# A new opening, other places for the modulation rows, and one update for all latents of a block

## The chip, the core and the metric

The kernel runs on one core of one Trainium2 chip. The metric is device time in microseconds (us) of one launch, the median of several executions. Engines are named as in the profile: PE is TensorE's matmul stream and PEld its weight loads, DVE is VectorE, ACT is ScalarE, POOL is GpSimd, and SP is the engine whose queue issues all DMAs of this kernel. L289 is line 289 of the kernel before.

## What is computed

Two layers of a diffusion backbone over 128 context tokens and 512 latent tokens, with a model width of 1024. Cut to what matters here:

```python
def ada_params(cvec, w_ada, b_ada):
    m = jax.nn.silu(cvec) @ w_ada + b_ada
    return jnp.split(m[:, None, :], 6, axis=-1)     # sh1, sc1, g1, sh2, sc2, g2

def modulate(x, g, shift, scale):
    return rms_norm(x, g) * (1 + scale) + shift

for l in range(DEPTH):
    sh1, sc1, g1, sh2, sc2, g2 = ada_params(c, w_ada[l], b_ada[l])
    h = modulate(x, norm_g[l, 0], sh1, sc1)
    y = mixer(h)                  # l = 0: pooling and gated convolution; l = 1: attention
    x = x + g1 * y
    h = modulate(x, norm_g[l, 1], sh2, sc2)
    x = x + g2 * swiglu(h, w_ffn_in[l], w_ffn_out[l])
```

Context tokens take one conditioning vector, latents another, so each modulation parameter has two columns.

## The kernel before, in words

Features lie on the 128 partitions, tokens along the free axis: `x` is 8 blocks (`k`) of 128 features by 640 columns, 128 of context and 512 of latents. Every fp32 product is made of three fp32r products: both operands are split by `pair` (L144, L145) into a high part (a copy on ACT) and a low part (the rest, on DVE), and hi·hi, hi·lo and lo·hi are summed in PSUM.

**Matmuls of a block.** `block_mm` (L283 to L296) makes one block of 128 output features. For each `k` and each of the three products it issues two matmuls with the same weights, one for columns 0 to 320 into one PSUM bank, one for columns 320 to 640 into the next bank. With `ext` (input projections) the second takes two more columns, the shift that goes through the weights with the tokens. Without `ext` it serves the output projections: `po` of layer 0, `wa` and `wb` of layer 1, and `fo` of both FFNs. The last two blocks of the last `fo` have a loop of their own (L1490), with all 384-column matmuls of a block first and then all 256-column ones, over the same `x` layout. The fast products of the FFN input (L632) put 12 matmuls of 320 columns one after the other into one bank.

**PSUM.** Blocks take turns in three PSUM tiles of two banks each, so a block's matmuls wait for what reads the block three turns before.

**Residuals.** When a block is done, `residual` and `update` (L508) add gate times block to `x[:, k]` with three DVE operations: context (128 columns), latents in the first bank (192) and latents in the second bank (320).

**Modulation parameters.** A part (shift, scale, gate; 8 blocks of 128) of layer 0 is made in one of two ways. In the opening, TensorE makes a chunk of 512 parameters from four DMAs of 512 KB of `w_ada` (`ada_pe`, L306: 16 matmuls with 2 columns of weights and 512 moving), ACT copies the result (L324), TensorE turns it (`ada_turn`, L330: 8 matmuls), and DVE adds the bias and makes the scale (L394, L403). All other blocks are rows of the class `AdaDve` (L372): per row one DMA of 512 KB and, on DVE, a multiply-and-sum with SiLU of the conditioning, `silb`. A row is two DVE pieces of 1024 elements in the mixer stage (`junk` in SBUF) and four of 512 in the FFN (`junk` in PSUM). Where rows are run is written by hand: `each` says how many rows go with a block. The first `EARLY` rows run in the opening, `pi` and `po`; 48 run in layer 0's FFN.

**The opening** (L774 to L904) is written by hand, in order, for every engine. Before, it loads the whole scale of layer 0's first norm (chunks 2 and 3), then half the shift (chunk 0); the other half of the shift is the first four rows on DVE. `prep` (L485, L487) makes bufA[k] = x[k] times scale. `first_mm` makes the first three blocks of `pi` as the pieces of `x` come. `nrm.finish` gives `rstd`, in two halves of columns. `scaled_main` (L523) takes a block out of PSUM as `ev`, `first_bias` and `first_turn` (L875, L888) add the shift to the first three blocks. `turn_over` (L815) is filler work on zeros. `ws.load` and `ws.split` load and split projection weights.

**Order.** Outside the opening a planner that knows the dependences orders each engine's work, by program order and readiness; a row is held behind the operation that was traced before it on its engine. `pi` is 16 blocks (3 in the opening, 13 in `project`), four for pooling (`s`, `pl`), twelve for the convolution. `po` is 8 blocks. Then comes the FFN in three groups (8, 8 and 6 hidden blocks, `gi` 0 to 2): input products, then 8 output blocks `fo` with rows beside them.

Of the kernel before, what the change touches and what calls it, by code (L numbers as in the profile page):

```python
# [36 lines left out]
EARLY = 28  # L37
# [23 lines left out]
def hybrid_step(  # L61
# [9 lines left out]
    wada0,  # L71
    wada,
# [209 lines left out]
    def block_mm(ps, w, rhs, kn, ext=False, mcol=0, k0=0, ks=None):  # L282
# [197 lines left out]
    def prep(k, dst, l, n):  # L480
        assert (l, 3 * n + 1, 4 if (l, 3 * n + 1, 4) in known and k < 4 else 8) in known
# [74 lines left out]
    def project(name, rhs, kn, n, done, ext=False, each=None, start=0):  # L556
        for i in range(start, n):
            ps = ps_tile(f"{name}_{i}")
            w = ws.next()
            if each:  # L560
                each(i)
            pipe.step(lambda: block_mm(ps, w, rhs, kn, ext=ext), lambda: done(i, ps))
# [192 lines left out]
    with tc.tile_pool(name="pool1", bufs=1) as p1:  # L755
# [6 lines left out]
        def ada_load(ch):  # L762
            for q in range(4):
                raw = p0.tile([P, 2, 512], F32, tag="araw", bufs=6, name=f"raw_ada{ch}_{q}")
                nc.sync.dma_start(raw, wada0[(ch + 1) // 2 if ch < 3 else 2, q])
                ada_raw.append(raw)
# [4 lines left out]
            [(0, 4, 4)]  # L771
            + [(0, 8 * p, 8) for p in (2, 4, 3)]
# [17 lines left out]
        ada.load()  # L790
        ada.load()
        pwr = p0.tile([P, 512], F32, tag="pwr", name="pwr").rearrange("p (g c) -> p g c", g=4)
        nc.sync.dma_start(pwr, pw)
        ws.load(3)
        zero = p0.tile([P, 512], F32, tag="junk", name="zero")
# [21 lines left out]
        turn_over(6)  # L817
        acc = {ch: ada_acc(ch) for ch in (2, 3)}
        ada_pe(2, acc[2], range(4))
        row = ada_row(2, acc[2])  # L820
        turn_over(3)
        ada_turn(2, row)
        turn_over(14)
        for k in range(4):
            prep(k, bufA, 0, 0)
            if k == 1:
# [4 lines left out]
        first_mm(0, range(4))  # L831
        ada_pe(3, acc[3], range(4))
        row = ada_row(3, acc[3])
        nrm.add_square(V)
        nrm.add_square(V)
        nrm.add_square(V)
        nrm.add_square(V)
        first_mm(1, range(2))
# [52 lines left out]
        first_mm(2, range(5, 6))  # L891
# [3 lines left out]
        first_mm(2, range(6, 8))  # L895
# [147 lines left out]
        for m in range(3):  # L1043
# [9 lines left out]
            each=lambda i: ada.run(1 + (5 <= i < 8)),  # L1053
# [19 lines left out]
        with tc.tile_pool(name="pool4", bufs=1) as p4:  # L1073
            ada.home(p4, p1, 2, ps_small("junk"), silb)
            ada.limit = len(ada.todo)
            ada.load()
            ada.load()
            more = tuple(p4.tile([P, 3 * 4 * HT], F32R, tag=t, name=t) for t in ("x0h", "x0l"))
            ffn(
                0,  # L1080
                bufA,
                bufA,
                each=lambda i, gi, plain=False: ada.run(0 if plain else 1 + (i % 2 if gi == 0 else int(i > 1))),
                fast_each=lambda gi, n, p: ada.run(int(p == 6 and gi > 0)),
                last=last0,
                spare=(tuple(t.rearrange("p a b -> p (a b)") for t in bufB), more),
            )
            assert ada.at == len(ada.todo)
# [4 lines left out]
    with tc.tile_pool(name="pool2", bufs=1) as p2:  # L1093
# [282 lines left out]
        def pieces(name, rhs, kn, todo, cuts, ext, done, share=1, k0=0):  # L1376
# [3 lines left out]
            def piece(i, c):  # L1380
# [5 lines left out]
                block_mm(box["ps"], box["w"], rhs, kn, ext, i % share, k0, range(c * n, c * n + n))  # L1386
# [57 lines left out]
        for m in range(2):  # L1444
            pipe.step(lambda: block_mm(fw[m], wpart[0], bufB, 4, mcol=m, k0=4, ks=range(3)))
        assert not pipe.due
        out_done = updater(1, 16, Norm("b1"), (bufA, 1, 1))
        for m in range(2):
            pipe.step(lambda: block_mm(fw[m], wpart[0], bufB, 4, mcol=m, k0=4, ks=(3,)), lambda: out_done(m, fw[m]))
        for m in range(2, KB):  # L1450
            if not m % 2:
# [3 lines left out]
                lambda: block_mm(ps, wpart[0], bufB, 4, mcol=m % 2, k0=4), lambda: out_done(m, ps)  # L1455
# [58 lines left out]
    gates = AdaDve([(1, 40 + b, 1) for b in range(8)], 76)  # L1514
# [59 lines left out]
_ADA_ORDER = [4, 5, 6, 7]  # L1574
_ADA_ORDER += [8 * p + b for p in (2, 4, 3, 5, 7, 6, 8, 10, 9, 11) for b in range(8)]
# [63 lines left out]
```

## Time and profile before

| | |
|---|---|
| median of 3 runs | 1356.52 us (1354.65 to 1358.49) |
| profiled execution, its own time | 1359.17 us |
| its span, first to last instruction | 1357.0 us |
| granted TensorE clock, mean | 0.993 of full |
| PE, DVE, ACT, POOL busy | 98, 79, 47 and 3% of the span |

Time stamps count from the first instruction. The opening ends at about 57 us, `pi` at 156.6, `po` at 213; layer 0's FFN ends at about 663, attention lies between 720 and 880, layer 1's FFN follows. A row of the timeline is start, duration, engine, line, operation, out<-in, shape and count; square brackets give the idle time of the engine before it and what ended it. Matmul ends are modelled and overlap the next start, so the pace of a stream is read from starts.

### The profile page before, as it was taken

The page shows a single profiled execution, that of the slowest core. Times are in us where ns is not written, and L with a number is a line of the kernel's source. Part 1 is how long each engine was busy: PE and PEld are TensorE (multiplying, and loading weights), DVE is VectorE, ACT ScalarE, POOL GpSimd, SP SyncE. Part 2 cuts the span into 40 slices and gives each one's busy share as a digit, 9 for nine tenths or more (in the row PEclk, how much of TensorE's full clock was granted, in tenths as well). Part 3 has the DMA queues.
Part 4 walks back from the last instruction along what each step waited for, and adds up shares of the span by engine and source line. Part 5 has one row for each costly group of instructions (what it writes and reads, how often), then busy time and mean ns, then how long its engine had stood idle before and what let it go on. Part 6 is the DMA issues. An engine that isn't in the chain of part 4 may idle for free.

```text
span 1357.0 us, 22469 instructions
## 1 busy us (share of the span) xinstructions
PE 1327.6 (98%) x8952; PEld 1295.8 (95%) x8952; DVE 1076.8 (79%) x2095; ACT 638.5 (47%) x1159; POOL 46.3 (3%) x56
## 2 busy tenths in 40 slices
PE   9999999999999999999999999999999999999996
PEld 6899999999999999999998999999999999999995
DVE  4899897978999999999877677599877777446744
ACT  5433245753145521554666675477541355314543
POOL 0000000000000000000012221000000000000001
PEclk9899999999999999999999999999999999999998
DMA  9735422115433454344431110141144122311212
GB/s 366 284 109 190 168 94 94 63 63 171 171 124 111 156 189 151 124 135 161 148 101 48 48 48 32 34 154 47 47 140 164 39 94 70 118 63 63 78 47 78
DMA packets 36808, 155.54 MB, mean 115 GB/s; under 512 B 3936, under 2 KB 11104, under 8 KB 25952
## 3 DMA queue, kind: packets, MB, share of 16 engines
q1 hardware_dynamic: 36704, 154.12, 32.8%
q8 instruction: 70, 1.15, 0.3%
q14 instruction: 34, 0.28, 0.1%
HBM read 148.60 MB, written 2.88 MB: 112 GB/s over the span
## 4 chain that ended last, share of the span: by engine, by line
PE 82%; DVE 11%; ACT 3%; issue 2%; DMA 1%; SPq 0%; POOL 0%; DVEq 0%; ACTq 0%; POOLq 0%
PE fi L632 28%; PE fo L289 19%; PE fi L289 8%; PE pi L289 7%; PE pq L289 5%; PE po L289 4%; DVE junk L372 3%; PE wb L289 2%; PE wa L289 2%; PE o L1355 2%; PE s L1305 2%; DVE wl_fi_p L145 1%; PE t L1338 1%; ACT wh_fi_p L144 1%; DMA x<-xT 1%
## 5 line engine op out<-in xcount | busy, mean ns | idle before, releaser
L144 ACT ACTIVATE wh_fi_p<-raw_fi 128x512 fp32r<-128x512 f32 x252 | 154.5, 626 | 232.0 <-PE fi L632 123.6
L372 DVE CUSTOM_DVE_ANT_0 junk<-rawa,silb 128x512 f32<-128x512 f32 (+1 forms) x280 | 224.1, 800 | 5.9 <-DMA rawa<-wada 1.7
L145 DVE TENSOR_TENSOR wl_fi_p<-raw_fi,wh_fi_p 128x512 fp32r<-128x512 f32 x252 | 171.4, 687 | 65.0 <-ACT wh_fi_p L144 65.0
L144 ACT ACTIVATE wh_fo<-raw_fo 128x1024 fp32r<-128x1024 f32 (+1 forms) x48 | 47.5, 990 | 147.4 <-PE fo L289 122.8
L508 DVE SCALAR_TENSOR_TENSOR x<-fo,mod,x 128x128 f32<-128x128 f32 (+1 forms) x144 | 55.8, 434 | 70.4 <-PE fo L289 67.2
L632 PE MATMUL fi<-bh,wh_fi_p 128*128 128x320 f32 x288 | 88.8, 308 | 1.8 <-DVE x L508 1.8
L632 PE MATMUL fi<-bh,wl_fi_p 128*128 128x320 f32 x288 | 88.9, 309 | 0.0
L632 PE MATMUL fi<-ah,wl_fi_p 128*128 128x320 f32 x288 | 88.7, 308 | 0.0
L632 PE MATMUL fi<-al,wh_fi_p 128*128 128x320 f32 x288 | 88.7, 308 | 0.0
L632 PE MATMUL fi<-ah,wh_fi_p 128*128 128x320 f32 x288 | 88.5, 307 | 0.0
L632 PE MATMUL fi<-bl,wh_fi_p 128*128 128x320 f32 x288 | 88.4, 307 | 0.0
L289 PE MATMUL fo<-al,wh_fo 128*128 128x320 f32 x352 | 80.8, 310 | 0.0
L289 PE MATMUL fo<-ah,wh_fo 128*128 128x320 f32 x352 | 80.6, 310 | 0.1
L289 PE MATMUL fo<-ah,wl_fo 128*128 128x320 f32 x352 | 80.4, 309 | 0.0
L289 PE MATMUL fo<-bh,wh_fo 128*128 128x320 f32 x328 | 75.2, 310 | 0.0
L289 PE MATMUL fo<-bh,wl_fo 128*128 128x320 f32 x328 | 75.0, 310 | 0.0
L289 PE MATMUL fo<-bl,wh_fo 128*128 128x320 f32 x328 | 74.9, 310 | 0.0
L632 PE MATMUL fi<-x0h,wh_fi_p 128*128 128x320 f32 x216 | 68.1, 320 | 1.5 <-ACT fi L644 0.9
L632 PE MATMUL fi<-xh,wh_fi_p 128*128 128x320 f32 x216 | 67.9, 320 | 0.2
L632 PE MATMUL fi<-xh,wl_fi_p 128*128 128x320 f32 x216 | 66.5, 309 | 0.0
L632 PE MATMUL fi<-xl,wh_fi_p 128*128 128x320 f32 x216 | 66.5, 309 | 0.0
L632 PE MATMUL fi<-x0h,wl_fi_p 128*128 128x320 f32 x216 | 66.4, 308 | 0.0
(372 smaller groups left out, 3786.7 us busy)
## 6 DMA issues: line engine op xcount, KB each, us to landing
raw_fi<-wfi SPq DMA_DIRECT2D x44, 1024.0 KB, 4.7
rawa<-wada SPq DMA_DIRECT2D x84, 512.0 KB, 3.4
raw_fo<-wfo SPq DMA_DIRECT2D x16, 1024.0 KB, 4.9
raw_ada<-wada SPq DMA_DIRECT2D x12, 512.0 KB, 7.3
raw_in<-win SPq DMA_DIRECT2D x6, 1024.0 KB, 5.3
raw_fo<-wfo SPq DMA_DIRECT2D x8, 768.0 KB, 4.2
raw_qkv<-wqkv SPq DMA_DIRECT2D x6, 1024.0 KB, 5.4
raw_out<-wout SPq DMA_DIRECT2D x4, 1024.0 KB, 5.2
```

Source lines behind the costliest of these rows:

```text
L144: S.activation(h, src, AF.Copy)
L145: eng.tensor_tensor(out=l, in0=src, in1=h.bitcast(F32), op=ALU.subtract)
L289: PE.matmul(ps[:, h, 0 : hi - lo], w[a][:, k, cols], rhs[b][:, k0 + k, lo:hi], start=k == 0 and a == b, stop=k == kn - 1 and a == 1,)
L372: op = V.tensor_tensor_reduce(out=self.junk, in0=raw[:, cols], in1=self.silb[:, c, cols], scale=1.0, scalar=0.0, op0=ALU.mult, op1=ALU.add ...
L508: V.scalar_tensor_tensor(out=xs, in0=got[:, 0 : b - a], scalar=mod[l][:, gate0 + m, c : c + 1], in1=xs, op0=ALU.mult, op1=ALU.add,)
L632: PE.matmul(out, w[a][:, k, :], ops.get(OPERAND[p], b)[:, k, :], start=fresh and k == 0 and a == b, stop=k == ops.kn - 1 and a == 1, skip_ ...
L1305: PE.matmul(self.ps[:, hf, 0:HT], bufB[a][:, self.h, q0 : q0 + P], kt[b][:, self.kv, hf * HT : hf * HT + HT], start=n == 0, stop=n == 2,)
L1338: PE.transpose(flat(pt)[:, s * P : s * P + P], self.pe[:, s * P : s * P + P], ident)
L1355: PE.matmul(po[:, 0 : 2 * P], vt[a][:, self.kv, s * P : s * P + P], got[b][:, s, :], start=s == 0 and n == 0, stop=s == 4 and n == 2,)
```

## The change

- The scale's first half (blocks 0 to 3) is made in two half chunks of 256 parameters, each from two DMAs (`wadah`, `ada_load_half`, `ada_half`, `ada_half_turn`), so `x` comes in pieces of 2, 2 and 4 blocks; the DMA order is new; win1 is loaded ahead of both shift chunks.
- The whole shift of layer 0's first norm is made on TensorE (chunks 0 and 1). The four rows on DVE are gone; `EARLY` is 24 instead of 28. SiLU of `silb` and the first two rows move to the end of the opening.
- `first_mm(2, ...)` is cut finer and partly moved ahead of the shift chunks.
- Rows with `pi`: 1, 0, 0, 1, 0, 1, 2, 1, 2, 1, 2, 1, 2 instead of 1, with 2 in the sixth to eighth. Rows with layer 0's `fo`: group 0 has 14 instead of 12, group 1 has 12 instead of 14, with 1 and 0 in its last two blocks instead of 2 and 2.
- Without `ext`, `block_mm` cuts at column 384 instead of 320, so each bank holds 256 latents, and `residual` updates all 512 latents with one DVE operation of two runs of 256.

```diff
-EARLY = 28
+EARLY = 24
+PI_ROWS = (1, 0, 0, 1, 0, 1, 2, 1, 2, 1, 2, 1, 2)
...
+    CUT = CTX + LAT // 2
-        span = ((0, 0, HT), (1, HT, TX if ext else T))
+        span = ((0, 0, cut), (1, cut, TX if ext else T))
...
     def residual(ps, m, l, gate0):
-        parts = ((0, 0, CTX, ps[:, 0]), (1, CTX, HT, ps[:, 0, CTX:]), (1, HT, T, ps[:, 1]))
-        update(m, l, gate0, parts)
+        update(m, l, gate0, [(0, 0, CTX, ps[:, 0])])
+        xs = halves(x[:, m, CTX:T])
+        V.scalar_tensor_tensor(
+            out=xs,
+            in0=flat(ps)[:, CTX : CTX + 768].rearrange("p (a b) -> p a b", a=2)[:, :, 0 : LAT // 2],
...
-        ada_load(2)
+        ada_load_half(0)
         nc.sync.dma_start(kc, konst)
-        nc.sync.dma_start(x[:, 0:4, :], xT[:, 0:4, :])
+        nc.sync.dma_start(x[:, 0:2, :], xT[:, 0:2, :])
         ws.load(1, cut=True)
+        ada_load_half(1)
+        nc.sync.dma_start(x[:, 2:4, :], xT[:, 2:4, :])
         ada_load(3)
         nc.sync.dma_start(x[:, 4:8, :], xT[:, 4:8, :])
+        ws.load(2, cut=True)
+        ada_load(0)
+        ada_load(1)
         nc.sync.dma_start(silb, crows[None].broadcast_to((P, 2, D)))
-        ada.load()
-        ada.load()
-        ada_load(0)
-        ws.load(2, cut=True)
-        ada.load()
-        ada.load()
         nc.sync.dma_start(pwr, pw)
         ws.load(3)
+        for _ in range(4):
+            ada.load()
...
-        turn_over(6)
-        acc = {ch: ada_acc(ch) for ch in (2, 3)}
-        ada_pe(2, acc[2], range(4))
-        row = ada_row(2, acc[2])
-        turn_over(3)
-        ada_turn(2, row)
-        turn_over(14)
-        for k in range(4):
+        turn_over(4)
+        row = ada_half(0)
+        turn_over(3)
+        ada_half_turn(0, row)
+        turn_over(10)
+        for k in range(2):
             prep(k, bufA, 0, 0)
...
+        first_mm(0, range(2))
+        row = ada_half(1)
+        first_mm(1, range(1))
+        ada_half_turn(1, row)
+        first_mm(1, range(1, 2))
+        for k in range(2, 4):
+            prep(k, bufA, 0, 0)
...
-        S.activation(silb, silb, AF.Silu)
+        ws.split(2, ahead=False)
...
-        ada.run(1, hold=False)
...
-        ada.run(1, hold=False)
-        ws.split(2, ahead=False)
-        ada.run(2, hold=False)
-        S.preload_act_table_set("natural_log_exp_and_others")
+        first_mm(2, range(0, 2))
         acc = ada_acc(0)
         ada_pe(0, acc, range(4))
         row = ada_row(0, acc)
+        S.preload_act_table_set("natural_log_exp_and_others")
+        first_mm(2, range(2, 3))
+        ada_turn(0, row)
         nrm.finish((0, HT), None)
-        first_mm(2, range(0, 1))
-        ada_turn(0, row)
-        first_mm(2, range(1, 5))
+        first_mm(2, range(3, 4))
+        acc = ada_acc(1)
+        ada_pe(1, acc, range(4))
+        row = ada_row(1, acc)
+        first_mm(2, range(4, 5))
+        ada_turn(1, row)
         prep_shift(bufA, 0, 0)
...
+        S.activation(silb, silb, AF.Silu)
         ws.split(4, ahead=False)
+        ada.run(2, hold=False)
         startup.close()
...
-            each=lambda i: ada.run(1 + (5 <= i < 8)),
+            each=lambda i: ada.run(PI_ROWS[i]),
...
-                each=lambda i, gi, plain=False: ada.run(0 if plain else 1 + (i % 2 if gi == 0 else int(i > 1))),
+                each=lambda i, gi, plain=False: ada.run(0 if plain else (1, 2, 1, 2, 2, 2, 2, 2)[i] if gi == 0 else (1, 2, 2, 2, 2, 2, 1, 0)[i]),
```

## Rows read from the trace of the kernel before

**Rows 1.** The page: busy time of each engine, share of the span, instructions.
```profile
PE 1327.6 (98%) x8952; PEld 1295.8 (95%) x8952; DVE 1076.8 (79%) x2095; ACT 638.5 (47%) x1159; POOL 46.3 (3%) x56
```
**Rows 2.** Waits of PE: who was waited for, us in total, times, longest.
```profile
PE pi L289 <- ACT ev L528: 2.1, 1, 2.1
PE fi L632 <- DVE x L508: 1.8, 1, 1.8
...
PE fi L632 <- ACT fi L644: 0.9, 1, 0.9
```
**Rows 3.** Busy time by stretch: length, each engine, granted clock (PEclk), DMA share, GB/s.
```profile
41.00:47.60 6.60, 6.60 (x27) 6.60 (x28) 6.36 (x14) 1.18 (x3) 0.00 (x0) 0.50 1.02 410
...
81.90:85.30 3.40, 3.40 (x15) 3.40 (x14) 3.40 (x7) 0.00 (x0) 0.00 (x0) 0.51 0.44 159
```
**Rows 4.** Timeline of the opening, PE.
```profile
24.31 0.95 PE L330 MATMUL adat<-kc,row 98*128 98x2 f32 x8
...
34.90 2.27 PE L306 MATMUL adap<-raw_ada,silc 128*2 128x512 f32 x16
...
38.97 0.55 PE L289 MATMUL pi<-ah,wh_in 128*128 128x320 f32 x2 [0.74 <-ACT wh_in L144]
...
40.90 0.90 PE L289 MATMUL pi<-ah,wl_in 128*128 128x320 f32 x2 [1.09 <-DVE wl_in L145]
```
**Rows 5.** Timeline from the opening to the third block of project, DVE and ACT.
```profile
29.34 1.90 ACT L843 ACTIVATE silb<-silb 128x2048 f32<-128x2048 f32 x1
...
38.93 1.28 ACT L856 ACT_TABLE_LOAD   x1
...
55.87 0.68 DVE L145 TENSOR_TENSOR bl<-pwr,bh 128x512 fp32r<-128x512 f32 x1
57.94 1.23 DVE L145 TENSOR_TENSOR wl_in<-raw_in,wh_in 128x1024 fp32r<-128x1024 f32 x1 [1.39 <-ACT wh_in L144]
...
67.80 1.22 DVE L372 CUSTOM_DVE_ANT_0 junk<-rawa,silb 128x1024 f32<-128x1024 f32 x1
...
79.79 0.82 DVE L523 TENSOR_TENSOR ev<-pi,rstd 128x640 f32<-128x640 f32 x1
```
**Rows 6.** Timeline of layer 0's FFN where a group's output ends, PE and DVE.
```profile
363.85 1.14 DVE L508 SCALAR_TENSOR_TENSOR x<-fo,mod,x 128x128 f32<-128x128 f32 x3 [1.32 <-PE fo L289]
...
377.78 0.31 PE L632 MATMUL fi<-bh,wh_fi_p 128*128 128x320 f32 x1
...
379.79 0.55 DVE L508 SCALAR_TENSOR_TENSOR x<-fo,mod,x 128x320 f32<-128x320 f32 x1
...
536.23 0.46 PE L626 MATMUL fi<-bh,onesr 128*128 128x320 f32 x2
...
539.57 0.55 DVE L508 SCALAR_TENSOR_TENSOR x<-fo,mod,x 128x320 f32<-128x320 f32 x1
```
**Rows 7.** The page: two groups, with busy us, mean ns, idle time before them.
```profile
L372 DVE CUSTOM_DVE_ANT_0 junk<-rawa,silb 128x512 f32<-128x512 f32 (+1 forms) x280 | 224.1, 800 | 5.9 <-DMA rawa<-wada 1.7
...
L508 DVE SCALAR_TENSOR_TENSOR x<-fo,mod,x 128x128 f32<-128x128 f32 (+1 forms) x144 | 55.8, 434 | 70.4 <-PE fo L289 67.2
```
**Rows 8.** Timeline of PE: first matmuls of streams of different width.
```profile
156.59 0.46 PE L289 MATMUL po<-bh,wh_out 128*128 128x320 f32 x2
...
213.24 0.46 PE L289 MATMUL fi<-ah,wh_fi 128*128 128x320 f32 x2
...
434.10 0.31 PE L632 MATMUL fi<-bh,wh_fi_p 128*128 128x320 f32 x1
...
437.60 0.36 PE L632 MATMUL fi<-bh,wh_fi_p 128*128 128x320 f32 x1
...
1331.80 0.34 PE L1490 MATMUL fo<-bh,wh_fo 128*128 128x384 f32 x1
...
1338.09 0.28 PE L1490 MATMUL fo<-bh,wh_fo 128*128 128x256 f32 x1
...
1340.10 0.28 PE L1490 MATMUL fo<-bh,wl_fo 128*128 128x256 f32 x1
```

More of the change, by code (lines that the diff above doesn't have):

```diff
@@ L71, in hybrid_step @@
     wada0,
+    wadah,
     wada,
@@ L480, in prep @@
     def prep(k, dst, l, n):
-        assert (l, 3 * n + 1, 4 if (l, 3 * n + 1, 4) in known and k < 4 else 8) in known
+        assert any((l, 3 * n + 1, m) in known for m in range(k + 1, 9))
         h, lo = dst
@@ L556, in project @@
     def project(name, rhs, kn, n, done, ext=False, each=None, start=0):
+        cut = HT if ext else CUT
         for i in range(start, n):
@@ L561, in project @@
                 each(i)
-            pipe.step(lambda: block_mm(ps, w, rhs, kn, ext=ext), lambda: done(i, ps))
+            pipe.step(lambda: block_mm(ps, w, rhs, kn, ext=ext, cut=cut), lambda: done(i, ps))
     def updater(l, gate0, nrm, then):
@@ L764, in ada_load, with ada_load_half @@
                 raw = p0.tile([P, 2, 512], F32, tag="araw", bufs=6, name=f"raw_ada{ch}_{q}")
-                nc.sync.dma_start(raw, wada0[(ch + 1) // 2 if ch < 3 else 2, q])
+                nc.sync.dma_start(raw, wada0[min(ch, 2), q])
+                ada_raw.append(raw)
+        def ada_load_half(half):
+            for q in range(2):
+                raw = p0.tile([P, 4, 256], F32, tag="araw", bufs=6, name=f"raw_adah{half}_{q}")
+                nc.sync.dma_start(raw, wadah[half, q])
                 ada_raw.append(raw)
@@ L815, in turn_over, with ada_half @@
                 PE.matmul(idle, zeror, zeror2, start=True, stop=True)
-        turn_over(6)
-        acc = {ch: ada_acc(ch) for ch in (2, 3)}
-        ada_pe(2, acc[2], range(4))
-        row = ada_row(2, acc[2])
+        half_acc = ada_acc("h")
+        def ada_half(half):
+            out = half_acc[:, 256 * half : 256 * half + 256]
+            for q in range(2):
+                raw = ada_raw.pop(0)
+                for j in range(4):
+                    PE.matmul(
+                        out[32 * j : 32 * j + 2, :],
+                        silc[:, 4 * q + j, :],
+                        raw[:, j, :],
+                        start=False,
+                        stop=q == 1,
+                        tile_position=(0, 32 * j),
+                        skip_group_check=True,
+                    )
+            row = tmp(f"rowh_{half}")[0:98, 0:256]
+            S.activation(row, out[0:98, :], AF.Copy)
+            return row
@@ new lines, in ada_half_turn @@
+        def ada_half_turn(half, row):
+            ps = ps_small(f"adath_{half}")
+            for b in range(2):
+                PE.matmul(
+                    ps[:, 2 * b : 2 * b + 2],
+                    row[:, b * P : b * P + P],
+                    kc[0:98, C_SUM : C_SUM + 2],
+                    start=True,
+                    stop=True,
+                )
+            ada_done(0, 8 + 2 * half, ps[:, 0:4].rearrange("p (b c) -> p b c", c=2))
+        turn_over(4)
+        row = ada_half(0)
@@ L829, in hybrid_step @@
         for k in range(4):
             nrm.square(k)
[L831 to L838, printed above, removed]
+        first_mm(0, range(2, 4))
+        acc = ada_acc(3)
+        ada_pe(3, acc, range(4))
+        row = ada_row(3, acc)
+        for _ in range(4):
+            nrm.add_square(V)
+        first_mm(1, range(2, 4))
@@ L1385, in piece @@
                 n = kn // cuts
-                block_mm(box["ps"], box["w"], rhs, kn, ext, i % share, k0, range(c * n, c * n + n))
+                block_mm(box["ps"], box["w"], rhs, kn, ext, i % share, k0, range(c * n, c * n + n), HT if ext else CUT)
                 if c == cuts - 1:
@@ L1444, in hybrid_step @@
         for m in range(2):
-            pipe.step(lambda: block_mm(fw[m], wpart[0], bufB, 4, mcol=m, k0=4, ks=range(3)))
+            pipe.step(lambda: block_mm(fw[m], wpart[0], bufB, 4, mcol=m, k0=4, ks=range(3), cut=CUT))
         assert not pipe.due
@@ L1448, in hybrid_step @@
         for m in range(2):
-            pipe.step(lambda: block_mm(fw[m], wpart[0], bufB, 4, mcol=m, k0=4, ks=(3,)), lambda: out_done(m, fw[m]))
+            pipe.step(lambda: block_mm(fw[m], wpart[0], bufB, 4, mcol=m, k0=4, ks=(3,), cut=CUT), lambda: out_done(m, fw[m]))
         for m in range(2, KB):
@@ L1454, in hybrid_step @@
             pipe.step(
-                lambda: block_mm(ps, wpart[0], bufB, 4, mcol=m % 2, k0=4), lambda: out_done(m, ps)
+                lambda: block_mm(ps, wpart[0], bufB, 4, mcol=m % 2, k0=4, cut=CUT), lambda: out_done(m, ps)
             )
@@ L1513, in hybrid_step @@
     S.activation(silb, silb, AF.Silu)
-    gates = AdaDve([(1, 40 + b, 1) for b in range(8)], 76)
+    gates = AdaDve([(1, 40 + b, 1) for b in range(8)], 72)
     gates.home(p3, p3, 2, ps_small("junk1"), silb)
@@ L1571 @@
 _FFN_ORDER = [b + j for j in range(FB) for b in (0, FB)]
-_ADA_ORDER = [4, 5, 6, 7]
-_ADA_ORDER += [8 * p + b for p in (2, 4, 3, 5, 7, 6, 8, 10, 9, 11) for b in range(8)]
+_ADA_ORDER = [8 * p + b for p in (2, 4, 3, 5, 7, 6, 8, 10, 9, 11) for b in range(8)]
 _SHAPES = (
```

33 lines of the change are left out of this document (18 added, 15 removed).

## The prediction, made before the change was run

> **What bounds the kernel now.** I read the busy times first: TensorE is busy for 98% of the span [rows 1]. So time is won only where TensorE waits, runs at its lower clock, or issues its stream at another pace; what VectorE (DVE) saves counts only where TensorE waits for it. Next, TensorE's waits by name [rows 2]: 2.1 us in the input projection for ACT's `ev`, 1.8 us in layer 0's FFN for the residual, 0.9 us beside it for ACT's `fi`. Then the stretches, for the granted clock [rows 3]: 0.50, its level of 1.2 GHz, from 41.0 to 47.6 us, and again from 81.9 to 85.3. Before each fall TensorE had waited: twice before the first [rows 4], 2.1 us at the projection's third block before the second. Last, the timelines around these places: a clock fall and a wait belong to the opening, and the two FFN waits stand where one group's output ends.
>
> **The opening, DMA order.** Up to chunk 3 the queue carries the same bytes in both kernels, only in other pieces, so `x[4:8]` comes when it came before. win1 is moved past silb, two rows and chunk 0, about 4.2 MB; at the 410 GB/s of a full queue [rows 3] it lands some 10 us earlier. Behind it, chunks 0 and 1, silb, pwr, win2 and four rows come later. Chunk 1's last two parts need buffers that TensorE frees in chunk 0, and all behind them on SP's queue wait too. I cost that at nothing: win2 is first needed by the second block of `project`, and pwr and the rows after the opening; if that cover goes, TensorE waits for win2 by the delay itself.
>
> **The opening, TensorE.** Gone are the waits for win1's parts, 0.74 + 1.09 = 1.8 us [rows 4], and with them the cause I see for the first clock fall: 6.60 us at half pace [rows 3] cost 3.3 us. The two half chunks stream as many columns as the chunk they replace. New is chunk 1 on TensorE: 2.27 us of matmuls and a turn of 0.95 [rows 4], 3.2 us. That leaves 1.9 us; up to 3.3 if finer pieces of `x` also hide the wait for chunk 3, which no row prices.
>
> **The opening, DVE and ACT.** I doubt that this gain reaches TensorE. The third block of `project` starts only when `ev` of its first convolution block is out of PSUM, and the row of that `ev` starts at 79.79 after DVE has been in arrears since the opening's end [rows 5]. The four shift rows that leave DVE ran before that, where DVE could spare them except beside win1. In their place SiLU of silb moves to the end, ahead of `wh_in` on ACT, with `wl_in` behind it on DVE: 1.90 us, and since ln and exp were loaded in between, a table load of 1.28 [rows 5], 3.2 us. Two rows, four pieces, also stand there, and one row comes with the first block: six pieces ahead of that `ev`, where the timeline has five, so 1.2 us more. Sum on this path: 3.2 + 1.2, less the 1.39 us that DVE idles there anyway [rows 5], less the 1.9 to 3.3 us that it starts earlier: +1.1 to -0.3 us, if the idle is filled. I take 0. Ends: -3.3, if nothing binds behind TensorE, and 3.2 + 1.2 - 1.9 = +2.5, if no idle is filled. The wait of 2.1 us grows to some 4 or 5 us, and I expect the second clock fall to stay.
>
> The Trainium skill (ScalarE: Activation LUTs, What ACT_TABLE_LOAD costs) speaks against this move: it puts a switch of table sets at 2.66 us, the load and a drain of 1.38. By it the opening would end 1.4 us later, and the sum would be -1.7 instead of -3.1; the row has the 1.28 us alone.
>
> **Rows beside `pi`.** 14 instead of 16 there and 2 instead of 4 in the opening. TensorE shows no wait for them in the later blocks, so 0; the cover is the three PSUM tiles. If DVE falls two blocks behind, a wait of up to a row's two pieces, 2.4 us [rows 5], comes back.
>
> **Rows in the FFN.** Group 1 loses two rows near its end, eight pieces of 0.80 [rows 7], 6.4 us of DVE. Its last residual ended at 540.12, 3.9 us after the output's last matmul [rows 6]; now it follows at once, and the waits of 1.8 and 0.9 us go [rows 2]: -2.7. Group 0 gets these two rows. Its last residual ended at 380.34, 2.6 us after the output [rows 6], and TensorE went on then without a wait. How late it gets is bounded twice: 6.4 us less the 1.32 that DVE idles there [rows 6], 5.1; or, by the group that has had 14 rows so far, 3.9 - 2.6 = 1.3. I take the second, the same blocks with the same number of rows, less about half for the shorter residuals: +0.6. Ends 0 and 5.1. Together -2.1.
>
> **One update.** It drops one of three operations whose busy time is 0.39 each (55.8/144) [rows 7], but moves the same elements, so 0 to 0.39 us per block. DVE is ahead of TensorE at these blocks but in the two places above, so 0 elsewhere.
>
> **The cut at 384.** This one touches most of the kernel: `fo`, `po`, `wa`, `wb`, 2808 matmuls, 1404 pairs, counted from the loops. The 384 matmuls of `po` take 213.24 - 156.59 = 56.65 us [rows 8], 147.5 ns each, 295.0 a pair. At L1490, 36 of 384 columns take 6.29 us, 174.7 each; 17 steps of 256 columns take 2.01, 118.2 each [rows 8]: 292.9 a pair, 2.1 ns less, -2.9 us over 1404. But those rows keep to one bank, and `block_mm` changes banks every time. In the fast products, which keep to one bank with 320 columns, 24 take 3.50 us, 145.8 each [rows 8], 291.6 for two: by them the new widths cost 1.3 ns a pair, +1.8 us. L1490 shares widths and layout with the changed blocks, the other stream does not, so I lean to it: -1.0, ends -2.9 and +1.8.
>
> The Trainium skill (TensorE: Matmul & The Clock Gate, Back-to-back issue gap) gives a gap of N/2.4 + 2.5 ns, 271.7 for either pair: by it the cut is worth 0 and the sum is -2.1. The rows are 8% slower than it, so it cannot decide a per cent.
>
> **Sum.** 0 - 2.1 - 1.0 = -3.1 us. The profiled execution took 1359.17 us, 2.17 more than its span; the start and end around the span don't change. 1359.17 - 3.1 = 1356.1. Its own time lies 2.65 above the median of the runs, so I give 1353.4 on the median's scale. 0.3%, about what a measurement of this kernel can tell from no change, is 4.1 us.
>
> **Rivals.**
> *The opening counts in full.* If the planner lays the two early rows behind the pool sums, DVE and ACT don't bind. For it: DVE loses a whole row in each of several blocks after. Against it: `ev` at 79.79. -3.3 - 2.1 - 1.0: 1350.1.
> *The FFN wait only moves.* Group 0's last residual has no slack, and 5.1 us late is a bound, so a wait of 2.7 there would cancel group 1's gain: 1355.5. Against it: group 1's own lateness.
> *Slower: the short half is bound by its weight load.* Each matmul reloads weights, and PEld is 95% busy [rows 1]. Behind a 384-column matmul the 256-column one may not keep 118.2 ns. From 295.0 - 174.7 + 1.5 = 121.8 ns the whole change loses; at 128 it is 9.8 above the row, and the time is 1359.17 - 2.65 - 2.1 + 1404 x 7.7 ns = 1365.2. Against it: L1490's stream keeps 118.2 for a whole block.
> *The clock falls in the new opening.* It feeds TensorE in pieces of two blocks, with waits for DMA between. The rows have a fall after such waits; one more of 6.6 us costs 3.3: 1356.7. The Trainium skill (TensorE: Matmul & The Clock Gate, HAM oscillation) says that idle gaps between bursts put the clock back to its lower level; the trace agrees, with 0.50 after the waits at 39 and 79 us.
>
> **Chances.** Forecast 0.48, opening in full 0.19, moved wait 0.17, short half 0.09, clock 0.07. Faster by over 0.3% means below 1352.4: the full opening and a third of the forecast, 0.36. Slower, above 1360.6: the short half, 0.09. Same: 0.55. The range, 1348.8 to 1358.0, takes in all but the short half and the far ends of the bounds: the low end is the full opening with part of the cut's -2.9, the high end the forecast with the opening at +2.5 and the cut at +1.1.
>
> **What would show it.** PE's waits: no L508 or `fi` wait near 536, one of under 1 us near 380, the one for `ev` L528 grown to 4 or 5 us. Clock: no fall near 41, one near 82. Pace: pairs of 384 and 256 at 294 ns. Wrong would be: `ev`'s wait no longer than 2.1 us, pairs under 292.9 or over 296.3, or a wait over 2 us after group 0.

## The result, and the profile after

The changed kernel takes 1361.17 us (median of 9 runs, 1359.86 to 1362.41), the kernel before 1358.07 beside it (9 runs, 1354.65 to 1359.38): ratio 1.0025, 95% interval 1.0016 to 1.0034. The forecast was 1353.4 us in a range of 1348.8 to 1358.0. So the change costs 3.4 us where 3.1 were to be won. (The forecast stood on a median of 1356.52 us from 3 runs; 1.6 us of its distance to the result lie in that base.) The profiled execution spans 1359.1 us, against 1357.0 before.

First the page, busy time by engine; then PE's waits (who was waited for, us in total, times, longest).

```profile
PE 1330.0 (98%) x8987; PEld 1298.0 (96%) x8987; DVE 1060.2 (78%) x2011; ACT 640.3 (47%) x1162; POOL 46.4 (3%) x56
```
```profile
PE py L1020 <- ACT ev L544: 2.8, 2, 2.6
...
PE pi L295 <- ACT ah L491: 2.0, 2, 1.5
PE pi L295 <- DVE bl L1029: 1.8, 1, 1.8
PE pi L295 <- DVE al L493: 0.5, 2, 0.2
...
PE fi L643 <- DVE x L528: 0.4, 1, 0.4
PE fi L649 <- ACT fi L661: 0.4, 1, 0.4
```

The FFN's waits of 1.8 and 0.9 us behind group 1 [rows 2] are gone; the 0.4 for `x` is new and stands behind group 0, the 0.4 for `fi` is new too, in layer 1's FFN at 965.81 us. In the projection one wait of 2.1 became two, 2.6 and 1.8. These two stand in PE's timeline, with the starts of `po` and of the FFN behind them, and the end of FFN group 0:

```profile
81.43 0.57 PE L1020 MATMUL py<-bh 128*128 128x320 f32 x2 [2.57 <-ACT ev L544]
...
84.85 0.90 PE L295 MATMUL pi<-ah,wh_in 128*128 128x320 f32 x2 [1.83 <-DVE bl L1029]
...
161.40 0.46 PE L295 MATMUL po<-bh,wh_out 128*128 128x384 f32 x2
...
218.08 0.45 PE L295 MATMUL fi<-ah,wh_fi 128*128 128x320 f32 x2
...
385.56 0.53 PE L643 MATMUL fi<-bh,onesr 128*128 128x320 f32 x2 [0.41 <-DVE x L528]
```

`po` starts at 161.40 where it started at 156.59 [rows 8]: 4.8 us are lost by then, and the rest of the kernel wins 2.7 of them back. How much of the 4.8 belongs to the opening itself shows in the start of its last turn, in the changed kernel and then before:

```profile
56.77 0.38 PE L946 MATMUL fturn<-kc,frow 4*128 4x2 f32 x2
```
```profile
56.37 0.38 PE L888 MATMUL fturn<-kc,frow 4*128 4x2 f32 x2
```

The new opening ends no earlier, and that holds beyond these two traces. That turn starts at 54.65 to 56.82 us, 55.6 on average, in the seven traces with the old opening (before, e1 to e4, e12, e14). It starts at 55.16 to 56.77, 56.1 on average, in the six with the new one unchanged up to there (the changed kernel, e5, e6, e13, e15, e17). So one execution's opening says little to a microsecond. The stretch from this turn to the start of `po` is steadier: 100.2 us in all six traces with the old opening and the old rows beside `pi`, 104.6 in the changed kernel. That stretch is where the change loses. The granted clock by stretch shows how the loss grows:

```profile
30.70:34.20 3.50, 3.50 (x15) 3.50 (x14) 3.36 (x5) 3.50 (x7) 0.00 (x0) 0.51 1.03 411
...
84.85:88.00 3.15, 3.15 (x12) 3.15 (x13) 3.15 (x5) 0.00 (x0) 0.00 (x0) 0.50 0.15 25
88.00:90.00 2.00, 2.00 (x13) 2.00 (x13) 2.00 (x4) 0.00 (x0) 0.00 (x0) 0.81 0.56 223
```

The fall near 41 us [rows 3] is gone, but there is one at 30.7, behind a wait of 1.50 for `ah`; the one near 82 now lasts to 88 and beyond. Last, DVE and ACT between the opening and those waits (some rows left out):

```profile
57.38 1.28 ACT L961 ACT_TABLE_LOAD   x1
58.67 1.92 ACT L961 ACTIVATE silb<-silb 128x2048 f32<-128x2048 f32 x1
```
```profile
61.56 1.23 DVE L148 TENSOR_TENSOR wl_in<-raw_in,wh_in 128x1024 fp32r<-128x1024 f32 x1 [4.37 <-ACT wh_in L147]
62.71 1.22 DVE L378 CUSTOM_DVE_ANT_0 junk<-rawa,silb 128x1024 f32<-128x1024 f32 x1
...
80.30 0.82 DVE L539 TENSOR_TENSOR ev<-pi,rstd 128x640 f32<-128x640 f32 x1
...
83.92 0.88 DVE L1029 SCALAR_TENSOR_TENSOR bl<-py,sm,bh 128x640 fp32r<-128x640 f32 x1
```

Names for what follows: pi_0 to pi_12 are the 13 blocks of `project`, py_0 to py_3 the products of the pool branches. They take the three PSUM tiles in turn: pi_0, pi_1, pi_2, then py_0 in the tile of pi_0, pi_3 in that of pi_1, pi_4 in that of py_0. The `ev` at 80.30 is that of pi_0, with six row pieces ahead of it; pi_1's follows at 90.05 behind eight. The planner put most of pi_4 ahead of pi_3 on PE, so the second wait is for py_0's eviction.

### The profile page after: what moved, and what is told of

Read it like the earlier page. It is cut to its first block, busy times and chain, and to the rows that moved or that the text cites. A ratio compares the mean times of both kernels' runs of the same rounds, so it can differ in the third digit from the quotient of the medians.

```text
span 1359.1 us, 22464 instructions
## 1 busy us (share of the span) xinstructions
PE 1330.0 (98%) x8987; PEld 1298.0 (96%) x8987; DVE 1060.2 (78%) x2011; ACT 640.3 (47%) x1162; POOL 46.4 (3%) x56
## 4 chain that ended last, share of the span: by engine, by line
PE 83%; DVE 12%; ACT 2%; issue 2%; DMA 0%; POOL 0%; DVEq 0%; SPq 0%; ACTq 0%; POOLq 0%
PE fi L649 28%; PE fo L295 18%; PE fi L295 8%; PE pi L295 7%; PE pq L295 5%; PE po L295 4%; DVE junk L378 4%; PE wb L295 2%; PE wa L295 2%; PE o L1415 2%; PE s L1365 2%; DVE wl_fi_p L148 1%; PE t L1398 1%; DVE wl_fo L148 1%; PE fo L1550 1%
## 5 line engine op out<-in xcount | busy, mean ns | idle before, releaser
L378 DVE CUSTOM_DVE_ANT_0 junk<-rawa,silb 128x512 f32<-128x512 f32 (+1 forms) x272 | 214.2, 787 | 4.2 <-DMA rawa<-wada 1.0
L295 PE MATMUL fo<-al,wh_fo 128*128 128x384 f32 (+1 forms) x352 | 81.0, 311 | 0.0
L295 PE MATMUL fo<-ah,wh_fo 128*128 128x384 f32 x352 | 80.8, 311 | 0.1
L295 PE MATMUL fo<-ah,wl_fo 128*128 128x384 f32 x352 | 80.5, 310 | 0.0
L295 PE MATMUL fo<-bh,wh_fo 128*128 128x384 f32 x328 | 75.2, 310 | 0.0
L295 PE MATMUL fo<-bh,wl_fo 128*128 128x384 f32 (+1 forms) x328 | 75.1, 310 | 0.0
L295 PE MATMUL fo<-bl,wh_fo 128*128 128x384 f32 x328 | 75.0, 310 | 0.0
L514 DVE SCALAR_TENSOR_TENSOR x<-fo,mod,x 128x128 f32<-128x128 f32 (+1 forms) x52 | 18.5, 359 | 72.2 <-PE fo L295 68.7
L649 PE MATMUL fi<-x0l,wh_fi_p 128*128 128x320 f32 x216 | 66.4, 308 | 0.0
```

Source lines behind the costliest of these rows:

```text
L295: PE.matmul(ps[:, h, 0 : hi - lo], w[a][:, k, cols], rhs[b][:, k0 + k, lo:hi], start=k == 0 and a == b, stop=k == kn - 1 and a == 1,)
L378: op = V.tensor_tensor_reduce(out=self.junk, in0=raw[:, cols], in1=self.silb[:, c, cols], scale=1.0, scalar=0.0, op0=ALU.mult, op1=ALU.add ...
L514: V.scalar_tensor_tensor(out=xs, in0=got[:, 0 : b - a], scalar=mod[l][:, gate0 + m, c : c + 1], in1=xs, op0=ALU.mult, op1=ALU.add,)
L649: PE.matmul(out, w[a][:, k, :], ops.get(OPERAND[p], b)[:, k, :], start=fresh and k == 0 and a == b, stop=k == ops.kn - 1 and a == 1, skip_ ...
```

## Experiments

All ratios are to the kernel before, measured beside the run; 0.0010 is 1.4 us. Theory A: the new opening loses what the rest wins. Its rivals are in the expectations.

### The parts alone (e1 to e4, e12)

e1 is the kernel before with all of the change but the opening and the rows beside `pi`, e2 with the FFN's rows alone, e3 with the cut alone:

```diff
-        span = ((0, 0, HT), (1, HT, TX if ext else T))
+        span = ((0, 0, cut), (1, cut, TX if ext else T))    # cut = 384 without ext
-        parts = (..., (1, CTX, HT, ps[:, 0, CTX:]), (1, HT, T, ps[:, 1]))
+        parts = (..., (1, CTX, CUT, ps[:, 0, CTX:]), (1, CUT, T, ps[:, 1]))
```

> The kernel before with all of the change but its opening: the new FFN rows, the cut at 384, the one update. Theory A (the new opening loses what the rest wins: the TensorE milestones of the two traces stand 4.8 us apart at the start of the output projection): 1.5 to 2.5 us below the kernel before, ratio 0.9982 to 0.9989. Theory B (the opening only shifts a wait and the loss lies in the later parts, cut and FFN rows together): no faster than before, ratio 1.000 to 1.002.

> The kernel before with the new places of the rows in the first FFN alone. Theory A: the waits of 1.8 and 0.9 us behind group 1 go and one of 0.4 to 0.9 us appears behind group 0: 2.0 to 2.6 us faster, ratio 0.9981 to 0.9985. Theory B (the rows only move the wait): within 0.5 us of before.

> The kernel before with the cut at 384 alone, the latents still updated by two operations. Theory A (a pair of 384 and 256 takes 295.6 to 297.5 ns instead of 295.1, as in the changed kernel's trace): 0.7 to 1.2 us slower, ratio 1.0005 to 1.0009. Theory B (what the prediction took, 294.3 ns a pair): 1.0 us faster.

> The same kernel once more with the latents of a block updated by one operation.

By a slip the kernel that ran as e4 was that of e3 once more, without the one update; it is a second measurement of the cut. e12 is what e4 was to be: e3 with the new `residual`.

> The kernel before with the cut at 384 and the latents of a block updated by one operation (what e4 was to be). Theory A (one update is worth 0, since VectorE is ahead of TensorE at these blocks but in two places): as e3 and e4, ratio 1.0005 to 1.0015. Rival (it shortens the wait behind the FFN's groups): 0.4 to 0.8 us below them.

| run | median us | ratio | interval |
|---|---|---|---|
| e1 old opening and rows beside `pi`, rest new | 1357.30 | 0.9994 | 0.9985 to 1.0003 |
| e2 FFN rows | 1356.47 | 0.9985 | 0.9976 to 0.9994 |
| e3 cut | 1359.42 | 1.0010 | 1.0001 to 1.0019 |
| e4 cut again | 1359.68 | 1.0011 | 1.0002 to 1.0020 |
| e12 cut and one update | 1356.88 | 0.9995 | 0.9986 to 1.0005 |

Everything but the opening and the rows beside `pi` is worth -0.8 us (e1), the whole change +3.4: these two cost 1.0025 - 0.9994 = 0.0031, 4.2 us. That is theory A, though e1 won less than the 1.5 us expected. Where it went shows in e1's DVE and PE at the end of FFN group 0:

```profile
371.72 0.70 DVE L374 CUSTOM_DVE_ANT_0 junk<-rawa,silb 128x512 f32<-128x512 f32 x1 [0.90 <-DMA rawa<-wada]
...
381.47 0.53 PE L639 MATMUL fi<-bh,onesr 128*128 128x320 f32 x2 [2.15 <-DVE x L524]
```

Behind the old opening the two added rows do make group 0 late, by 2.15 us; in the changed kernel the same place waits 0.41. e2's trace has a wait of 1.38 us there too: its FFN waits only fall from 1.8 + 0.9 to 1.4 + 0.3 + 0.2, and the time from the start of `po` to the end from 1200.4 to 1199.8 us, less than the 2.0 us of its runs (interval 0.8 to 3.3). In e1 a row's DMA came 0.90 late, behind a weight load on the queue.

The cut costs about 1.5 us, the interval says 0.1 to 2.6. In the traces the time from the start of `po` to the end grows by less, from 1357.0 - 156.6 = 1200.4 us to 1358.0 - 157.0 = 1201.0 in e3. One update takes the two runs of the cut, 0.0010 and 0.0011, to -0.0005, some 2 us, more than its rival expected; the intervals just overlap. From the start of `po` to the end it is 1200.2 us in e12, 0.8 to 1.0 less than in e3 and e4. PE's timeline behind group 1, of e4 and then of e12, shows a wait that is 1.2 us shorter:

```profile
539.98 0.39 PE L635 MATMUL fi<-bh,wh_fi_p 128*128 128x320 f32 x1 [1.80 <-DVE x L510]
```
```profile
538.01 0.39 PE L645 MATMUL fi<-bh,wh_fi_p 128*128 128x320 f32 x1 [0.64 <-DVE x L524]
```

### Undoing parts of the opening (e5 to e8)

```diff
e5: two rows from the opening's end to pi_7 and pi_9
-PI_ROWS = (1, 0, 0, 1, 0, 1, 2, 1, 2, 1, 2, 1, 2)
+PI_ROWS = (1, 0, 0, 1, 0, 1, 2, 2, 2, 2, 2, 1, 2)
         ws.split(4, ahead=False)
-        ada.run(2, hold=False)
e6:
-        S.activation(silb, silb, AF.Silu)
         ws.split(4, ahead=False)
+        S.activation(silb, silb, AF.Silu)
e7:
         ada_turn(3, row)
+        turn_over(4)
e8: all three
```

> The changed kernel without its two rows at the end of the opening; they are run beside the blocks pi_7 and pi_9 instead. Theory A (the rows and the SiLU at the opening's end put VectorE in arrears, and TensorE waits 2.6 + 1.8 us for it behind pi_2): four pieces of 1.2 us go from ahead of ev(pi_0), the wait of 2.6 us goes and the second shrinks: 2.5 to 4.5 us below the changed kernel, so 1356.7 to 1358.7 us. Theory B (the loss of the opening lies earlier, in chunk 1 on TensorE and in the clock's fall at 29 us, and VectorE's queue only shifts): less than 1 us below it, and the wait comes back a block or two later.

> The changed kernel with one swap: the SiLU of silb, with its table load, stands behind the weight split ws.split(4) on ACT instead of ahead of it. Theory A: wh_in comes 3.2 us earlier, VectorE's idle of 4.4 us before wl_in falls to about 1.2, and the rows alone wait for SiLU: 1 to 3 us below the changed kernel. Theory B: less than 1 us below it, since the rows still stand ahead of ev(pi_0).

> The changed kernel with four idle matmuls on TensorE behind the turn of chunk 3, where it waits 1.5 us for ah. Theory A (the fall of the clock from about 31 to 34 us follows that wait and costs half its length): no stretch at 0.50 there, TensorE 1.3 to 2 us earlier at the opening's end, and 1 to 2 us below the changed kernel. Rival: the clock falls all the same, or VectorE and ACT set the end and the gain is eaten: within 0.5 us.

> The changed kernel with the three edits of e5, e6 and e7 together. Theory A: they undo most of the loss of the opening, 4 to 6 us below the changed kernel, 1355 to 1357 us. Theory B: 1 to 2 us below it, from the clock alone.

| run | median us | ratio | interval |
|---|---|---|---|
| e5 no early rows | 1353.48 | 0.9970 | 0.9958 to 0.9981 |
| e6 SiLU behind the split | 1359.31 | 1.0009 | 1.0000 to 1.0017 |
| e7 idle matmuls | 1359.92 | 1.0016 | 1.0007 to 1.0025 |
| e8 all three | 1353.07 | 0.9968 | 0.9957 to 0.9979 |

The two rows are 7.5 us of the result, more than theory A gave them, and without them the time, 4.1 us below the kernel before, is near the forecast. In e5, ev(pi_0) comes 6.8 us earlier, PE waits once, and the clock stays up:

```profile
73.48 0.82 DVE L539 TENSOR_TENSOR ev<-pi,rstd 128x640 f32<-128x640 f32 x1
```
```profile
79.94 0.56 PE L295 MATMUL pi<-ah,wh_in 128*128 128x320 f32 x2 [2.04 <-DVE bl L1028]
...
154.07 0.46 PE L295 MATMUL po<-bh,wh_out 128*128 128x384 f32 x2
```
```profile
79.90:82.00 2.10, 2.06 (x14) 2.07 (x15) 2.10 (x4) 0.00 (x0) 0.00 (x0) 1.00 0.32 129
82.00:86.00 4.00, 4.00 (x29) 4.00 (x29) 4.00 (x10) 0.91 (x2) 0.17 (x3) 1.00 0.38 131
```

Of the 7.3 us between the two starts of `po`, the row pieces explain 2.57 + 1.83 - 2.04 = 2.4 us of waits and about 2 us of half pace from 84.85 to 90 (3.15 x 0.50 + 2.00 x 0.19); 1.3 us stood already at the opening's end, whose last turn starts at 56.77 and 55.48, in code that is the same: that is the spread between executions, and 6.0 us (104.6 against 98.6) belong to the stretch behind it. The remaining 1.6 is in waits of 0.3 and less, in py_0 at half pace, and in rows that I did not add up.

e6 gives 2.2 us (the intervals touch), as theory A had it; in its trace the stretch from the last turn to `po` is 0.8 us shorter, and DVE idles 1.14 us ahead of `wl_in` and 2.00 more for SiLU, where it idled 4.37. e7 gives 1.2 us by the medians, with intervals that overlap. Its trace has no stretch at half pace in the opening, but the one behind pi_2 stands as before, `po` starts at 161.7, and the last turn at 57.00, no earlier than in the changed kernel, where 1.3 to 2 us were expected. Nor is it shown that the idle matmuls keep the clock up: e13's trace has no such stretch without them, and e18's has one with them (granted clock 0.62 from 28 to 32 us).

```profile
30.00:36.00 6.00, 6.00 (x41) 5.88 (x41) 5.65 (x9) 5.07 (x9) 0.00 (x0) 1.00 0.84 336
...
84.00:90.00 6.00, 4.92 (x20) 4.92 (x21) 6.00 (x10) 0.00 (x0) 0.00 (x0) 0.56 0.23 87
```

e8 is no faster than e5 beyond the noise, so what e6 and e7 won does not add to e5's gain.

### Place or number of the rows (e9, e13 to e16)

e9 keeps both rows in the opening, in DVE's idle stretch at 37 us:

```diff
+        nc.sync.dma_start(silb, ...)      # ahead of ada_load(0), ada_load(1), with two ada.load()
...
+        S.activation(silb, silb, AF.Silu)  # behind the squares of x[4:8]
         for _ in range(4):
             nrm.add_square(V)
+        ada.run(2, hold=False)
...
-        S.activation(silb, silb, AF.Silu)
         ws.split(4, ahead=False)
-        ada.run(2, hold=False)
```

> The changed kernel with the two rows kept in the opening but put where VectorE idles: silb and the two rows come ahead of chunks 0 and 1 on the DMA queue, SiLU runs before ln and exp are loaded (so without a second table load), the rows behind the squares of x. Theory A (what costs is the place of the rows and of SiLU, between the opening's end and ev(pi_0), not the work): 5 to 8 us below the changed kernel, 1353 to 1356 us, as without the rows. Rival (the two rows are too much for VectorE wherever they stand, or the later chunks 0 and 1 cost TensorE as much in waits): less than 3 us below it.

It took 1361.97 us, ratio 1.0033 (1.0021 to 1.0045): the theory of the place fell as I had put it. The stretch that the rows left does get shorter, 101.6 us from the last turn to `po` instead of 104.6. But the opening gives that back: ev(pi_0) is in time, yet PE waits longer, now for ev(pi_1), since here the planner left pi_3 ahead of pi_4; and the opening's last turn starts at 58.84, 2.1 us later.

```profile
85.03 0.90 PE L295 MATMUL pi<-ah,wh_in 128*128 128x320 f32 x2 [3.77 <-ACT ev L544]
```

e13 has one row at the opening's end; e14 is e1 with the rows of e5 beside `pi`, that is one fewer beside pi_1, pi_2, pi_4 and pi_5 and one more beside pi_8, pi_9, pi_10 and pi_12; e15 is e5, and e16 is e8, with pi_0's row moved to pi_11.

> The changed kernel with one row at the end of its opening instead of two; the other is run beside pi_7. Theory A (each of VectorE's pieces ahead of ev(pi_0) and ev(pi_1) costs TensorE its 1.2 us once the slack is used, and the clock's fall costs the rest): between e5 and the changed kernel, 1355 to 1359 us. Rival (a jump by VectorE's order or by the clock): at one of the two, within 1 us of 1353.5 or of 1361.2.

> The kernel of e1 (the old opening with the rest of the change) with the rows beside pi placed as in e5: five fewer rows beside pi_1 to pi_5, four more beside pi_8 to pi_12 and one fewer in all but the last. Theory A (the new opening saves TensorE some 3 us as soon as VectorE keeps up): as e1, within 1 us, since the old opening's own wait of 2.1 us for ev(pi_1) may go but its clock falls stay; e5 stays 2 us or more ahead. Rival (what e5 gained over e1 is the later rows and not the opening): as e5, ratio to the kernel before about 0.997.

> The kernel of e5 with the row beside pi_0 moved to pi_11 as well, so that the first row after the opening is beside pi_3. Theory A: VectorE has two pieces, 2.4 us, less ahead of the eviction that TensorE still waits 2.0 us for, and that wait goes: 1 to 2 us below e5, ratio to the kernel before 0.9955 to 0.9965. Rival (that wait is for py_0's own chain and not for the rows): as e5.

> The kernel of e8 with the rows of e15: the sum of what has helped. Theory A: 1351 to 1352.5 us, ratio to the kernel before 0.995 to 0.996. Rival: as e8, 0.9968.

| run | median us | ratio | interval |
|---|---|---|---|
| e13 one early row | 1357.66 | 1.0008 | 0.9999 to 1.0017 |
| e14 old opening, later rows | 1359.64 | 1.0018 | 1.0009 to 1.0027 |
| e15 as e5, first row beside pi_3 | 1355.12 | 0.9979 | 0.9970 to 0.9988 |
| e16 as e8, first row beside pi_3 | 1356.26 | 0.9994 | 0.9985 to 1.0003 |

e13 lies between: 1361.2, 1357.7 and 1353.5 us for two, one and no row at the opening's end, so there the price goes with the number, though not evenly: by the ratios the first row taken away wins 2.3 us and the second 5.2, and from the last turn to `po` it is 104.6, 102.4 and 98.6 us. In e13 the clock still falls behind the waits, in e5 it does not. e14 answers what e5's gain belongs to: later rows behind the old opening lose 3.3 us against e1, so e5's lead of 0.0024, 3.3 us, over e1 comes only with the new opening. The traces don't put that lead at the opening's end (55.48 in e5, 55.37 in e1): 1.6 us stand between there and `po`, and 1.9 behind the start of `po`, where e1 has its wait of 2.15 behind group 0 and e5 one of 0.42. But e15 and e16 deny that fewer pieces are always better. In e16 PE waits 4.05 us for ev(pi_1), with two pieces ahead of it. In e15 it waits less than in e5, and the clock falls behind it all the same:

```profile
80.55 0.57 PE L295 MATMUL pi<-ah,wh_in 128*128 128x320 f32 x2 [1.80 <-DVE bl L1028]
```
```profile
79.90:82.00 2.10, 1.45 (x8) 1.45 (x9) 2.10 (x5) 0.00 (x0) 0.00 (x0) 0.85 0.61 238
82.00:86.00 4.00, 4.00 (x20) 4.00 (x20) 4.00 (x9) 2.16 (x6) 0.17 (x3) 0.65 0.00 0
```

### What holds `ev` back (e17, e18)

In the traces ev(pi_0) stands right behind `pl` of the second pool branch, and in the changed kernel sums of the third branch, three weight splits and the row pieces go ahead of that `pl`. `ev`, the pool sums and `pl` take their tiles from the same eight buffers. e17 changes one line of the changed kernel, e18 the same line of e8:

```diff
-                nxt = tmp(f"s_{g}_{w}")
+                nxt = p0.tile([P, UL], F32, tag="sum", bufs=2, name=f"s_{g}_{w}")
```

> The changed kernel with one line changed: the pool sums take their tiles from two buffers of their own instead of the eight that they share with ev, up, pl and the rest. Theory A (ev of pi_0 and pi_1 waits for a buffer that the pool sums hold, and the rows delay the sums): ev(pi_0) and ev(pi_1) come one pool branch earlier, the waits of 2.6 and 1.8 us shrink to less than 2 us together, 3 to 7 us below the changed kernel (1354 to 1358 us), with the two rows where they were. Rival (VectorE's sum of work decides, in whatever order): within 1.5 us of the changed kernel.

> The kernel of e8 with the sums' own two buffers. Theory A: the wait of 1.8 us left for py_0's eviction goes too: 1 to 2 us below e8, ratio to the kernel before 0.9953 to 0.9961. Rival: as e8, 0.9968, or slower if a clock fall comes in.

e17 takes 1358.00 us, ratio 1.0000 (0.9991 to 1.0009): 3.4 us less than the changed kernel, with both rows where they were. With two buffers of their own the third branch's sums wait their turn, `pl` and ev(pi_0) behind it come earlier, at 74.54 with four pieces ahead, and PE's wait of 2.6 is gone; 3.2 us for py_0's eviction are left, more than the 2 that theory A allowed. In the traces the stretch from the last turn to `po` is 1.7 us shorter, 103.0 against 104.6.

```profile
74.54 0.81 DVE L539 TENSOR_TENSOR ev<-pi,rstd 128x640 f32<-128x640 f32 x1
```
```profile
PE pi L295 <- DVE bl L1029: 3.2, 1, 3.2
```

e18 takes 1353.09 us, 0.9966 (0.9952 to 0.9979), no better than e8; its wait is 1.33, for ev(pi_1), instead of 1.8.

### Without the cut, and the order of the banks (e10, e11)

e10 is e8 with the cut at 320 and the old `residual`; e11 adds:

```diff
-            for a, b in THREE:
-                for h, lo, hi in span:
+            for h, lo, hi in span:
+                for a, b in THREE:
```

> The kernel of e8 with the cut back at 320 and the latents updated by two operations. If the cut costs its pairs' pace here too: 0.5 to 1.5 us below e8, 1351.5 to 1352.6 us. If a shorter residual is worth more than that: above e8.

> The kernel of e10 with the three products of one half issued one after the other in block_mm, so that TensorE changes the PSUM bank every third matmul instead of every one. Theory (a matmul that changes the bank takes 147.5 ns instead of the 145.8 of the fast products, 320 columns each): two of three matmuls of some 4900 gain 1.5 to 1.7 ns, 5 us below e10. Rival (the pace belongs to the stream's operands and layout, not to the bank): no change.

e10 takes 1352.41 us, 0.9966 (0.9954 to 0.9979), e11 1352.29, 0.9967 (0.9954 to 0.9979). The cut and the one update cancel; the order of the banks is worth nothing. The source view of `po` (times of one, first and last start) has 56.5 us from the first start of the stream to the last in both, e10 first:

```profile
L295 PE MATMUL po<-bh,wh_out x128: 307/310/316, 153.7 to 209.6; 128*128 128x320 f32 x128
...
L295 PE MATMUL po<-bh,wl_out x128: 304/310/317, 154.3 to 210.2; 128*128 128x320 f32 x128
```
```profile
L295 PE MATMUL po<-bh,wh_out x128: 304/311/315, 153.6 to 209.8; 128*128 128x320 f32 x128
...
L295 PE MATMUL po<-bh,wl_out x128: 307/310/314, 153.8 to 210.1; 128*128 128x320 f32 x128
```

e5, e8, e10, e11 and e18 beat the kernel before by 4 to 5 us and the changed one by some 8, and can't be told apart.

## Why the prediction was wrong

**The opening is the step that failed.** It stood in the sum at 0, with +2.5 as its upper end; with the rows beside `pi` it cost 4.2. Four of its sub-steps gave way.

- "Less the 1.9 to 3.3 us that it starts earlier." Nothing behind the opening starts earlier: its last turn is at 56.77 us instead of 56.37, and thirteen traces say the same. The 1.8 us of waits for win1 went, but 2.5 us for `ah` and `al` came (0.50, 0.23, 1.50, 0.23). The 1.50 stands behind the turn of chunk 3, until DVE has made the scale (27.19) and ACT the first `ah` (27.59); before, TensorE still had matmuls of `pi` to do at that place. The fall of 6.6 us at half pace went, but one of 3.5 came. And 3.3 us was that fall's dearer case: from 40 to 50 us the mean granted clock is 0.66 in three traces of the old opening (before, e3, e14) and 0.83 in four (e1, e2, e4, e12), so the same code lost 3.4 or 1.7 of these 10 us.
- "Six pieces ahead of that `ev`, where the timeline has five, so 1.2 us more." The six pieces were counted rightly and set against the wrong `ev`. [Rows 5] ends with ev(pi_1) at 79.79, which pi_3, the fourth block of `project`, waits for; the six stand ahead of ev(pi_0), which had two ahead of it before. So it was four pieces more, 4.9 us instead of 1.2, for the block whose tile py_0 needs first. Before, that `ev` was here:

```profile
70.90 0.82 DVE L523 TENSOR_TENSOR ev<-pi,rstd 128x640 f32<-128x640 f32 x1
```

It comes 9.4 us later, at 80.30: 4.9 for the pieces, 3.0 for the longer idle of the next point, 0.6 for the later end of the opening, and 0.9 for the order of the rest. e13 and e5, which take the rows away one by one, bear the price out.

- "Less the 1.39 us that DVE idles there anyway", and 0 "if the idle is filled". The idle grew to 4.37, since SiLU and its table load stand on ACT ahead of the weights that DVE waits for. e6 puts 2.2 us on it.
- The wait was priced as a wait. It brought a stretch at 1.2 GHz, about 2 us, where e5 has none. The Trainium skill (TensorE: Matmul & The Clock Gate, HAM oscillation) tells of waits for DMA between bursts of matmuls that put the clock back to its lower level. The changed kernel and e15 agree as far as the clock fell behind such waits, to 0.50 and 0.65; in e5 and e8 it stayed at 1.00 behind waits of 2.04 and 1.80 us.

The signs that the prediction named did not catch this, for they came true: no wait near 536, 0.41 near 380, the waits in the projection grown to 2.6 + 1.8 = 4.4 us, no fall near 41 and one near 82. The longer wait was to be paid for by an earlier start, and none of the signs measured that start.

Behind the last three points stands the order on DVE, and that hangs on buffers: e17 gives back 3.4 us (1.7 in its trace's stretch to `po`) without touching a row. The prediction saw PSUM's three tiles as the cover and did not look at the eight buffers that `ev` shares with the pool sums. That `ev` waits for one of them is my reading; what e17 shows is what their assignment is worth.

**Gone with the first clock fall** were 3.3 us, the prediction said. The fall near 41 did go, and the rival that had the clock fall in the new opening, given 0.07, came true as well, at 30.7 us. The two, 6.6 and 3.5 us at half pace, leave 1.6 us of the 3.3. Whether e7's 1.2 us, within the intervals, come from the second fall is open, as said there.

**The rival "opening counts in full"** priced the gain at 3.3 us, and that is what e5 wins over e1. That is luck: the rival's 3.3 lay in an earlier end of the opening, and e5 wins half of its lead in the projection and half behind group 0 of the FFN.

**FFN rows:** -2.1 forecast, -2.0 measured alone (e2). In the changed kernel the mechanism held: 2.7 us of waits gone, 0.41 new behind group 0. In e2's trace the new wait is 1.38, and 0.6 us are won from the start of `po` to the end; in e1 it is 2.15. So behind the old opening the rival "the FFN wait only moves" is half right, and how it splits between groups depends on what came before the FFN.

**One update** stood at 0, and e12 puts it near -2 us with the old FFN rows, by intervals that just overlap, and at -0.8 to -1.0 by the traces. The step counted an operation's 0.39 us. The planner lays a row piece of 0.7 us between a block's updates, so one update less also takes a piece out of the way of the last one.

**The cut** had the wrong sign: -1.0 forecast, +1.5 measured, +0.6 in the trace. The step that failed is "I lean to it", to the stream at L1490. `po` takes 218.08 - 161.40 = 56.68 us for its 192 pairs, 295.2 ns a pair, against 295.0 before and the 292.9 of L1490. The reason given for the difference, that `block_mm` changes banks every time, is not the cause: e11 changes them a third as often, with 320 columns, at the same pace. What sets the pace is open. The rival of a short half bound by its weight load is not what happened either; it wanted over 296.5 ns a pair.

**Still open:** what decides whether the clock falls behind some 2 us of waiting; what holds the new opening's end where the old one's was, since no run takes its waits for `ah` and `al` away by themselves; and why the planner runs pi_4 ahead of pi_3 in some of these kernels and not in others. In e9 and e16 that goes with waits of 3.8 and 4.1 us, but no run changes it alone.

## What to carry to other kernels

Work put behind a hand-ordered opening is to be counted against the first block that must leave PSUM after it, not against the block that waited in the old trace. Ask what else that eviction needs; here it may be a buffer shared with a slow branch. One trace is one execution: the same opening ended up to 2.2 us apart, so price a wait or a clock fall from several, and look for the gain at the place where it is said to arise. Where a planner orders the rest, measure each small move of filler work: two rows in other places made it -4.1 us (e5) or +4.5 (e9, with SiLU moved too) against the kernel before.

## What was not expected of the hardware

After waits of 2.04 us (e5) and 1.80 (e8) the clock stayed at 1.00, after one of 1.80 for the same eviction it fell (e15). The table load took 1.28 us and SiLU began at once behind it, at 58.67; the Trainium skill (ScalarE: Activation LUTs, What ACT_TABLE_LOAD costs) counts a drain of 1.38 us on top, 2.66 in all, which no row here has. And 320-column matmuls keep 147 ns a piece in `po` whether the PSUM bank changes every matmul or every third.
